# Whole-batch loads of 8 MB through three fixed buffers in a batched row-product and softmax kernel

## The chip, the cores and the metric

The kernel runs on one core of one Trainium2 chip. The metric is the device time of one execution in microseconds (us), the median of several. The profile's span is about 2 us shorter than that time. VectorE is called DVE in the profile's lines, ScalarE ACT, GpSimd POOL, and SP is the engine whose queue issues the loads (SPq).

## The reference

```python
B, N, D = 8, 4096, 512                       # x, y: (B, N, D) float32, 64 MiB each
gram = np.matmul(x, y.transpose(0, 2, 1))
diag = np.diagonal(gram, axis1=1, axis2=2)   # one product-sum over D per row
diag = diag - diag.max(axis=-1, keepdims=True)
exp = np.exp(diag)
return exp / exp.sum(axis=-1, keepdims=True) # softmax over the N rows of a batch
```

Only the diagonal is wanted, so each row of x is multiplied with the same row of y and summed. The 134.22 MB of input are read once.

## The kernel before

A batch lies in SBUF, the memory on the chip that the engines read, as 128 partitions of 32 rows. The kernel works in half batches: 16 rows of x and 16 of y, each a 4 MB load that gives every partition one run of 32 KB. Three x tiles and three y tiles rotate.

```python
H = R // 2                                             # R = 32 rows per partition
io = ctx.enter_context(tc.tile_pool(name="io", bufs=3))
...
def load(b, r0, parts):
    xt = io.tile([P, H, D], f32, tag="xt", name="xt")
    yt = io.tile([P, H, D], f32, tag="yt", name="yt")
    ...
        nc.sync.dma_start(out=xt[:, o : o + n, :], in_=xv[b, :, r0 + o : r0 + o + n, :])
        nc.sync.dma_start(out=yt[:, o : o + n, :], in_=yv[b, :, r0 + o : r0 + o + n, :])
...
def dots(b, r0, xt, yt):
    nc.vector.tensor_tensor(out=xt, in0=xt, in1=yt, op=mybir.AluOpType.mult)
    nc.vector.tensor_reduce(out=diag[:, c : c + H], in_=xt, axis=X, op=add)
...
for b in range(B):
    for h in range(2):
        parts = {2 * B - 2: [8, 8], 2 * B - 1: [8, 4, 2, 1, 1]}.get(n, [H])
        xt, yt = load(b, h * H, parts)
        (dots_by_row if n >= 2 * B - 3 else dots)(b, h * H, xt, yt)
    softmax(b)                                         # after every batch, in DVE's order
```

`dots_by_row` makes one fused multiply-and-sum per row. `softmax` takes the maximum on DVE, reduces it over the partitions on POOL, exponentiates on ACT, sums on POOL, scales on DVE and stores the batch from ACT's queue.

## Time and profile before

| | before |
|---|---|
| time, median (range) | 323.7 us (323.36 to 323.76, 3 runs) |
| load queue, share of the 16 DMA engines' span | 97.5% |
| mean rate over the span | 418 GB/s |
| DVE busy | 81% |

The lines below are from the page of the kernel before. The rows of digits and rates are the span in 40 slices of 8 us.

```profile
span 321.6 us, 345 instructions
DVE 261.4 (81%) x154; ACT 4.6 (1%) x17; POOL 6.1 (2%) x20
...
DVE  0019979898998979979799897989979799776494
...
DMA  8999999999999999999999999999999999999991
GB/s 326 456 395 452 440 408 456 391 458 391 456 412 436 454 395 456 440 408 458 416 432 456 392 458 440 408 456 417 433 449 395 456 437 412 424 424 426 427 407 53
...
q1 hardware_dynamic: 6048, 134.22, 97.5%
```

The DMA row is 9 from the second slice to the one before last: the DMA engines never run dry. The queue line (packets, MB, share) gives 6048 packets. In the trace's DMA records, a packet of 32 KB takes 1213 ns, so 16 engines can carry 16 x 32768 B / 1213 ns = 432 GB/s. The Trainium skill ("DMA: Bandwidth & Descriptors", Where 436 GB/s comes from) puts the ceiling of the 16 SBUF ports at 435.2 GB/s; the trace agrees within 1%. There is little to win here except packet overhead and the two edges.

Why the queue never runs dry is seen from the next lines: the sizes and the median time from issue to landing (the moment when the last of the 16 engines has reported its part done) of the 4 MB loads, and the issues of SP's queue in a stretch of the timeline (start us, us).

```profile
xt<-in_x_dram SPq DMA_DIRECT2D x14, 4096.0 KB, 31.2
yt<-in_y_dram SPq DMA_DIRECT2D x14, 4096.0 KB, 40.5
```

### The profile page before, as it was taken

How to read it: one execution, taken by the hardware profiler on the slowest of the kernel's cores; microseconds unless marked ns; L12 is line 12 of the kernel's file. 1: busy time of each engine (PE TensorE's matmuls, PEld its weight loads, DVE VectorE, ACT ScalarE, POOL GpSimd, SP SyncE). 2: the span in 40 equal slices, each digit the busy share in tenths (PEclk: the TensorE clock that was granted, in tenths of full speed). 3: DMA queues.
4: the chain of work that ended last, by engine and by line, in shares of the span. 5: the costliest groups of instructions: out<-in, count | busy, mean ns of one | idle time of the engine just before them, and what ended most of it. 6: DMA issues, size and time to landing. Idle time of an engine off the chain costs nothing.

```text
span 321.6 us, 345 instructions
## 1 busy us (share of the span) xinstructions
DVE 261.4 (81%) x154; ACT 4.6 (1%) x17; POOL 6.1 (2%) x20
## 2 busy tenths in 40 slices
DVE  0019979898998979979799897989979799776494
ACT  1000000000000000000000000000000000000000
POOL 0000000000000000000000000000000000000000
DMA  8999999999999999999999999999999999999991
GB/s 326 456 395 452 440 408 456 391 458 391 456 412 436 454 395 456 440 408 458 416 432 456 392 458 440 408 456 417 433 449 395 456 437 412 424 424 426 427 407 53
DMA packets 7201, 134.36 MB, mean 418 GB/s; under 512 B 1824, under 2 KB 1824, under 8 KB 2592
## 3 DMA queue, kind: packets, MB, share of 16 engines
q1 hardware_dynamic: 6048, 134.22, 97.5%
q10 hardware_dynamic: 1152, 0.13, 0.3%
q14 instruction: 1, 0.01, 0.0%
HBM read 134.22 MB, written 0.13 MB: 418 GB/s over the span
## 4 chain that ended last, share of the span: by engine, by line
DMA 63%; DVE 33%; issue 1%; SPq 1%; POOL 1%; ACT 0%; POOLq 0%; DVEq 0%
DMA yt<-in_y_dram 63%; DVE xt L50 16%; DVE diag L51 16%; SPq L43 1%; POOL mx L74 0%; POOL ssum L83 0%; DVE mxp L72 0%; DVE xt L58 0%; ACT res L78 0%; DVE rc L85 0%; POOLq L121 0%; SPq L44 0%; DVE res L86 0%; DVE nmx L76 0%; DVEq L50 0%
## 5 line engine op out<-in xcount | busy, mean ns | idle before, releaser
L50 DVE TENSOR_TENSOR xt<-xt,yt 128x8192 f32<-128x8192 f32 x13 | 113.0, 8689 | 34.5 <-DMA yt<-in_y_dram 34.5
L51 DVE TENSOR_REDUCE diag<-xt 128x16 f32<-128x8192 f32 x13 | 112.9, 8686 | 0.4
L58 DVE SCALAR_TENSOR_TENSOR xt<-xt,yt 128x512 f32<-128x512 f32 x48 | 30.0, 687 | 9.9 <-DMA yt<-in_y_dram 9.7
L74 POOL PARTITION_ALL_REDUCE mx<-mxp x8 | 2.8, 352 | 306.6 <-DVE mxp L72 306.6
L85 DVE RECIPROCAL rc<-ssum 128x1 f32<-128x1 f32 x8 | 1.3, 164 | 7.7 <-POOL ssum L83 7.7
L78 ACT ACTIVATE res<-diag,nmx 128x32 f32<-128x32 f32 x8 | 2.6, 321 | 312.9 <-DVE nmx L76 312.9
L76 DVE TENSOR_SCALAR nmx<-mx 128x1 f32<-128x1 f32 x8 | 1.2, 154 | 4.3 <-POOL mx L74 4.3
L58 DVE DVE_READ_ACCUMULATOR xt<-xt,yt 128x1 f32 x48 | 3.9, 82 | 0.0
L83 POOL PARTITION_ALL_REDUCE ssum<-sump x8 | 3.1, 385 | 5.8 <-ACT res L78 5.8
L86 DVE TENSOR_SCALAR res<-res,rc 128x32 f32<-128x32 f32 x8 | 1.9, 242 | 0.9
L72 DVE TENSOR_REDUCE mxp<-diag 128x1 f32<-128x32 f32 x8 | 1.5, 186 | 0.3
L78 ACT ACTIVATION_READ_ACCUMULATOR res<-diag,nmx 128x1 f32 x8 | 1.5, 186 | 0.0
L78 ACT ACT_TABLE_LOAD x1 | 1.3, 1283 | 0.7 <-PEq L110 0.7
L110 POOL MEMSET const-float32-0.0<- 128x1 f32 x1 | 0.1, 100 | 0.2 <-issue 0.2
L110 POOL MEMSET const-bfloat16-1.0<- 128x1 bf16 x1 | 0.1, 102 | 0.0
L110 POOL MEMSET const-uint8-127<- 128x1 uint8 x1 | 0.1, 102 | 0.0
L110 POOL MEMSET const-float32-1.0<- 128x1 f32 x1 | 0.1, 99 | 0.0
## 6 DMA issues: line engine op xcount, KB each, us to landing
xt<-in_x_dram SPq DMA_DIRECT2D x14, 4096.0 KB, 31.2
yt<-in_y_dram SPq DMA_DIRECT2D x14, 4096.0 KB, 40.5
xt<-in_x_dram SPq DMA_DIRECT2D x3, 2048.0 KB, 27.1
yt<-in_y_dram SPq DMA_DIRECT2D x3, 2048.0 KB, 31.6
xt<-in_x_dram SPq DMA_DIRECT2D x1, 1024.0 KB, 31.9
yt<-in_y_dram SPq DMA_DIRECT2D x1, 1024.0 KB, 29.5
xt<-in_x_dram SPq DMA_DIRECT2D x1, 512.0 KB, 25.8
yt<-in_y_dram SPq DMA_DIRECT2D x1, 512.0 KB, 22.2
```

The lines of the kernel that those rows point to most:

```text
L43: nc.sync.dma_start(out=xt[:, o : o + n, :], in_=xv[b, :, r0 + o : r0 + o + n, :])
L50: nc.vector.tensor_tensor(out=xt, in0=xt, in1=yt, op=mybir.AluOpType.mult)
L51: nc.vector.tensor_reduce(out=diag[:, c : c + H], in_=xt, axis=mybir.AxisListType.X, op=mybir.AluOpType.add)
L58: nc.vector.scalar_tensor_tensor(out=xt[:, k, :], in0=xt[:, k, :], scalar=1.0, in1=yt[:, k, :], op0=mybir.AluOpType.mult, op1=mybir.AluOpT ...
L72: nc.vector.tensor_reduce(out=mxp, in_=db, axis=mybir.AxisListType.X, op=mybir.AluOpType.max)
L74: nc.gpsimd.partition_all_reduce(out_ap=mx, in_ap=mxp, channels=P, reduce_op=bass_isa.ReduceOp.max)
L76: nc.vector.tensor_single_scalar(out=nmx, in_=mx, scalar=-1.0, op=mybir.AluOpType.mult)
L78: nc.scalar.activation(out=rb, in_=db, func=mybir.ActivationFunctionType.Exp, bias=nmx, scale=1.0, accum_out=sump,)
L83: nc.gpsimd.partition_all_reduce(out_ap=ssum, in_ap=sump, channels=P, reduce_op=bass_isa.ReduceOp.add)
L85: nc.vector.reciprocal(out=rc, in_=ssum)
L86: nc.vector.tensor_single_scalar(out=rb, in_=rb, scalar=rc, op=mybir.AluOpType.mult)
L110: nc = _bacc.Bacc("TRN2", target_bir_lowering=False, num_devices=1)
```

## The change

The intent is longer runs (64 KB per partition, hence fewer packets), fewer instructions, and no softmax stalls in DVE's order. Whole batches of 8 MB go through three fixed buffers of 64 KB per partition: two for x, one for y. The product overwrites x. Two whole batches of both operands would be 256 KB per partition; the change keeps to the 192 KB that the six tiles took before, so y has only one buffer. The softmax of batches 0 to 4 and of 5 and 6 is done in groups. Batches 6 and 7 are done by row.

```diff
-    H = R // 2
+    wide = B - 2
...
-    io = ctx.enter_context(tc.tile_pool(name="io", bufs=3))
+    xs = [big.tile([P, R, D], f32, name=f"xs{i}") for i in range(2)]
+    ys = big.tile([P, R, D], f32, name="ys")
...
+    def load_x(b, r0, n):
+        nc.sync.dma_start(out=xs[b % 2][:, r0 : r0 + n, :], in_=xv[b, :, r0 : r0 + n, :])
+
+    def load_y(b, r0, n):
+        nc.sync.dma_start(out=ys[:, r0 : r0 + n, :], in_=yv[b, :, r0 : r0 + n, :])
+
+    def dots_wide(b):
+        xt = xs[b % 2]
+        nc.vector.tensor_tensor(out=xt, in0=xt, in1=ys, op=Alu.mult)
+
+    def sums_wide(b):
+        nc.vector.tensor_reduce(out=diag[:, b, :], in_=xs[b % 2], axis=X, op=Alu.add)
...  (group_exp, group_out, last_softmax: the softmax in groups, and of the last batch)
-    for b in range(B):
-        for h in range(2):
-            n = 2 * b + h
-            parts = {2 * B - 2: [8, 8], 2 * B - 1: [8, 4, 2, 1, 1]}.get(n, [H])
-            xt, yt = load(b, h * H, parts)
-            (dots_by_row if n >= 2 * B - 3 else dots)(b, h * H, xt, yt)
-        softmax(b)
+    for b in range(wide):
+        load_x(b, 0, R)
+        load_y(b, 0, R)
+        dots_wide(b)
+        if b == wide - 1:
+            group_out("a", 0, wide - 1, first)
+        sums_wide(b)
+        if b == wide - 2:
+            first = group_exp("a", 0, wide - 1)
+
+    b = B - 2
+    load_x(b, 0, R)
+    for r0 in (0, R // 2):
+        load_y(b, r0, R // 2)
+        for r in range(r0, r0 + R // 2):
+            dot_row(b, r)
+
+    b = B - 1
+    r0 = 0
+    for n in (8, 8, 8, 4, 2, 1, 1):
+        load_x(b, r0, n)
+        load_y(b, r0, n)
+        for r in range(r0, r0 + n):
+            if r == 2:
+                second = group_exp("b", B - 3, 2)
+            if r == 10:
+                group_out("b", B - 3, 2, second)
+            dot_row(b, r)
+        r0 += n
+    last_softmax(b)
```

More of the change, by code (lines that the diff above doesn't have):

```diff
@@ L19 @@
     nc = tc.nc
+    ctx.enter_context(tc.manual_schedule())
     f32 = mybir.dt.float32
+    Alu = mybir.AluOpType
+    Act = mybir.ActivationFunctionType
+    X = mybir.AxisListType.X
     B, N, D = x.shape
@@ L23 @@
     R = N // P
-    H = R // 2
+    wide = B - 2
     xv = x.rearrange("b (p r) d -> b p r d", p=P)
     yv = y.rearrange("b (p r) d -> b p r d", p=P)
-    ov = out.rearrange("b (p r) -> b p r", p=P)
-    io = ctx.enter_context(tc.tile_pool(name="io", bufs=3))
-    persist = ctx.enter_context(tc.tile_pool(name="persist", bufs=1))
-    sm = ctx.enter_context(tc.tile_pool(name="sm", bufs=2))
-    diag = persist.tile([P, B * R], f32, name="diag")
-    res = persist.tile([P, B * R], f32, name="res")
@@ L38, in load @@
-    def load(b, r0, parts):
-        xt = io.tile([P, H, D], f32, tag="xt", name="xt")
-        yt = io.tile([P, H, D], f32, tag="yt", name="yt")
-        o = 0
-        for n in parts:
-            nc.sync.dma_start(out=xt[:, o : o + n, :], in_=xv[b, :, r0 + o : r0 + o + n, :])
-            nc.sync.dma_start(out=yt[:, o : o + n, :], in_=yv[b, :, r0 + o : r0 + o + n, :])
-            o += n
-        return xt, yt
-    def dots(b, r0, xt, yt):
-        c = b * R + r0
-        nc.vector.tensor_tensor(out=xt, in0=xt, in1=yt, op=mybir.AluOpType.mult)
-        nc.vector.tensor_reduce(
-            out=diag[:, c : c + H], in_=xt, axis=mybir.AxisListType.X, op=mybir.AluOpType.add
-        )
@@ L55, in dots_by_row @@
-    def dots_by_row(b, r0, xt, yt):
-        for k in range(H):
-            c = b * R + r0 + k
-            nc.vector.scalar_tensor_tensor(
-                out=xt[:, k, :],
-                in0=xt[:, k, :],
-                scalar=1.0,
-                in1=yt[:, k, :],
-                op0=mybir.AluOpType.mult,
-                op1=mybir.AluOpType.mult,
-                accum_out=diag[:, c : c + 1],
-            )
-    def softmax(b):
-        db = diag[:, b * R : (b + 1) * R]
-        rb = res[:, b * R : (b + 1) * R]
-        mxp = sm.tile([P, 1], f32, tag="mxp", name="mxp")
-        nc.vector.tensor_reduce(out=mxp, in_=db, axis=mybir.AxisListType.X, op=mybir.AluOpType.max)
-        mx = sm.tile([P, 1], f32, tag="mx", name="mx")
-        nc.gpsimd.partition_all_reduce(out_ap=mx, in_ap=mxp, channels=P, reduce_op=bass_isa.ReduceOp.max)
-        nmx = sm.tile([P, 1], f32, tag="nmx", name="nmx")
-        nc.vector.tensor_single_scalar(out=nmx, in_=mx, scalar=-1.0, op=mybir.AluOpType.mult)
-        sump = sm.tile([P, 1], f32, tag="sump", name="sump")
-        nc.scalar.activation(
-            out=rb, in_=db, func=mybir.ActivationFunctionType.Exp,
-            bias=nmx, scale=1.0, accum_out=sump,
-        )
-        ssum = sm.tile([P, 1], f32, tag="ssum", name="ssum")
@@ new lines, with column @@
+    ov = out.rearrange("b (p r) -> p b r", p=P)
+    big = ctx.enter_context(tc.tile_pool(name="big", bufs=1))
+    small = ctx.enter_context(tc.tile_pool(name="small", bufs=1))
+    xs = [big.tile([P, R, D], f32, name=f"xs{i}") for i in range(2)]
+    ys = big.tile([P, R, D], f32, name="ys")
+    diag = small.tile([P, B, R], f32, name="diag")
+    res = small.tile([P, B, R], f32, name="res")
+    def column(name, n):
+        return small.tile([P, n], f32, name=name)
+    def load_x(b, r0, n):
+        nc.sync.dma_start(out=xs[b % 2][:, r0 : r0 + n, :], in_=xv[b, :, r0 : r0 + n, :])
@@ new lines, in load_y, with dot_row @@
+    def load_y(b, r0, n):
[5 more added lines that the diff above has]
+        nc.vector.tensor_reduce(out=diag[:, b, :], in_=xs[b % 2], axis=X, op=Alu.add)
+    def dot_row(b, r):
+        xt = xs[b % 2]
+        nc.vector.scalar_tensor_tensor(
+            out=xt[:, r, :],
+            in0=xt[:, r, :],
+            scalar=1.0,
+            in1=ys[:, r, :],
+            op0=Alu.mult,
+            op1=Alu.mult,
+            accum_out=diag[:, b, r : r + 1],
+        )
@@ new lines, in group_exp @@
+    def group_exp(name, b0, n):
+        mxp, mx, nmx, sump, ssum = (column(name + s, n) for s in ("mxp", "mx", "nmx", "sump", "ssum"))
+        nc.vector.tensor_reduce(out=mxp, in_=diag[:, b0 : b0 + n, :], axis=X, op=Alu.max)
+        nc.gpsimd.partition_all_reduce(out_ap=mx, in_ap=mxp, channels=P, reduce_op=bass_isa.ReduceOp.max)
+        nc.scalar.mul(nmx, mx, -1.0)
+        for i in range(n):
+            nc.scalar.activation(
+                out=res[:, b0 + i, :], in_=diag[:, b0 + i, :], func=Act.Exp,
+                bias=nmx[:, i : i + 1], scale=1.0, accum_out=sump[:, i : i + 1],
+            )
+        nc.gpsimd.partition_all_reduce(out_ap=ssum, in_ap=sump, channels=P, reduce_op=bass_isa.ReduceOp.add)
+        return ssum
@@ new lines, in group_out, with last_softmax @@
+    def group_out(name, b0, n, ssum):
+        rc = column(name + "rc", n)
+        nc.vector.reciprocal(out=rc, in_=ssum)
+        for i in range(n):
+            rb = res[:, b0 + i, :]
+            nc.scalar.activation(out=rb, in_=rb, func=Act.Copy, scale=rc[:, i : i + 1])
+        nc.scalar.dma_start(out=ov[:, b0 : b0 + n, :], in_=res[:, b0 : b0 + n, :])
+    def last_softmax(b):
+        db, rb = diag[:, b, :], res[:, b, :]
+        mxp, mx, nmx, sump, ssum, rc = (column("l" + s, 1) for s in ("mxp", "mx", "nmx", "sump", "ssum", "rc"))
+        nc.vector.tensor_reduce(out=mxp, in_=db, axis=X, op=Alu.max)
+        nc.gpsimd.partition_all_reduce(out_ap=mx, in_ap=mxp, channels=P, reduce_op=bass_isa.ReduceOp.max)
+        nc.vector.tensor_single_scalar(out=nmx, in_=mx, scalar=-1.0, op=Alu.mult)
+        nc.scalar.activation(out=rb, in_=db, func=Act.Exp, bias=nmx, scale=1.0, accum_out=sump)
@@ L83, in softmax @@
         nc.gpsimd.partition_all_reduce(out_ap=ssum, in_ap=sump, channels=P, reduce_op=bass_isa.ReduceOp.add)
-        rc = sm.tile([P, 1], f32, tag="rc", name="rc")
         nc.vector.reciprocal(out=rc, in_=ssum)
-        nc.vector.tensor_single_scalar(out=rb, in_=rb, scalar=rc, op=mybir.AluOpType.mult)
-        nc.scalar.dma_start(out=ov[b], in_=rb)
-    for b in range(B):
-        for h in range(2):
-            n = 2 * b + h
-            parts = {2 * B - 2: [8, 8], 2 * B - 1: [8, 4, 2, 1, 1]}.get(n, [H])
-            xt, yt = load(b, h * H, parts)
-            (dots_by_row if n >= 2 * B - 3 else dots)(b, h * H, xt, yt)
-        softmax(b)
+        nc.vector.tensor_single_scalar(out=rb, in_=rb, scalar=rc, op=Alu.mult)
@@ new lines, in last_softmax @@
+        nc.scalar.dma_start(out=ov[:, b, :], in_=rb)
+    for b in range(wide):
[14 more added lines that the diff above has]
+    b = B - 1
```

## The prediction

> **What bounds the kernel now.** The load queue. The queue table gives 134.22 MB at 97.5% of the 16 DMA engines' span of 321.6 us. In the DMA records a 32 KB packet takes 1213 ns (median), a 16 KB packet 612 ns: 601 ns per 16 KB plus about 11 ns per packet, so 16 engines carry 16 x 32768 B / 1213 ns = 432 GB/s. The Trainium skill ("DMA: Bandwidth & Descriptors", Where 436 GB/s comes from) names a 435.2 GB/s port ceiling; the trace agrees. In stretches of 10 us the DMA share is 0.97 to 1.07 from 10 us to about 310 us: there is no hole to fill. The chain of waits reads the same way: DMA yt 63%; the DVE pieces in it (33%) only freed buffers whose loads queued behind others. VectorE is busy 81% and waits for yt 44 us.
>
> Edges: first packet 1.4 us after the first issue; last y piece lands at 316.1, then one row, softmax and store to 321.6 (timeline). The call adds 2.1 us.
>
> **What the change does.**
> 1. Bytes: the same; 8.39 MB per DMA engine at 601 ns per 16 KB is 307.7 us. That floor is not touched.
> 2. Packets: about 336 per DMA engine before, about 232 after (64 KB for six and a half batches). At 11 ns each, 1.2 us saved, all on the critical path, if a 64 KB run travels as one packet.
> 3. Three buffers, one y. Estimates: multiply and sum over 16384 elements take 2 x 8.69 minus 0.15 = 17.2 us each. y(b+1) can be issued only when multiply b ends, 17.3 us after y(b) landed, and its first packet follows 1.3 to 1.45 us later (last store and first load): at 18.65 to 18.75. x(b+1) keeps the DMA engines busy until 18.9 to 19.3 (19.33 us per 8 MB; engines finish within 0.43 us of each other). So y arrives just in time, with 0.2 to 0.6 us to spare. I expect holes of 0 to 0.5 us at six handovers: 1 us in total. x(b+1) waits for sums b-1, and is 4 us early.
> 4. Batches 6 and 7 by row: 64 rows at a pace of 0.612 us (timeline) are 39.2 us. After y(5), VectorE needs 34.6 + 39.2 + about 1 = 75 us; the loads need about 78. The end stays DMA-bound, with 3 us of slack.
> 5. Softmax groups: eight in-order stalls of about 2.3 us leave VectorE, but it was waiting for DMA anyway. The last softmax and store are the same.
>
> **Sum.** 321.6 - 1.2 + 1 = 321.4 us of span, about 323.2 us. Predicted 323.0 us, 80% range 321.0 to 326.5. Faster by over 2%: 2%; within 2%: 93%; slower by over 2%: 5%.
>
> **What would show each step.** Load packets falling from 6048 to about 4200, with 64 KB packets near 2415 ns; if runs are cut in two, no saving. Load queue share 97 to 98%, 418 to 420 GB/s. Each y issue 17.3 us after the previous y landing, x-to-y gaps under 0.5 us in the packet starts. y(5) landing near 236 us, last y near 315 to 316. VectorE waiting only for DMA at the end.
>
> **What would make it wrong.** An idle DMA engine that restarts slowly: the program's first packets took up to 1.95 us instead of 1.21; such a restart at six handovers would cost 5 us. A wait for a whole y buffer instead of its rows in batch 7 would cost 15 us or more. GpSimd reductions delayed by VectorE, so that a reciprocal blocks the row products. VectorE later than estimated at the end, making the tail compute-bound.

## More of the kernel before

Every run named here is a fast one at a granted clock of 1.0.

```profile
176.61 0.33 SPq L43 DMA_DIRECT2D xt<-in_x_dram  x1
177.03 0.38 SPq L44 DMA_DIRECT2D yt<-in_y_dram  x1
196.32 0.33 SPq L43 DMA_DIRECT2D xt<-in_x_dram  x1
196.70 0.42 SPq L44 DMA_DIRECT2D yt<-in_y_dram  x1
```

A 4 MB load needs 9.7 us of the DMA engines' time, but it takes 31 to 41 us from issue to landing: it stands in the queue behind two or three others. That is about 20 to 30 us of work ahead of every load. A late multiply cannot be felt.

## The result

| | before | after |
|---|---|---|
| time, median (range) | 323.65 us (323.36 to 323.76, 4 runs) | 331.65 us (330.63 to 332.73, 4 runs) |
| ratio | | 1.0249 (1.0216 to 1.0282) |
| load packets | 6048 | 4176 |
| load queue share | 97.5% | 95.5% |

A ratio is the mean time of one kernel's fast runs over that of the other's of the same rounds, so it is not quite the ratio of the medians. The changed kernel is 2.5% slower, outside the predicted range of 321.0 to 326.5 us.

The page of the kernel after, the lines that answer to those of before:

```profile
span 331.0 us, 298 instructions
DVE 247.6 (75%) x148; ACT 6.2 (2%) x26; POOL 3.3 (1%) x10
...
DVE  0000099992999949999399983999829999999584
...
DMA  9898998998999898899999899898999799999992
GB/s 380 380 507 380 451 436 380 388 491 388 483 396 388 380 499 388 380 436 444 396 459 396 380 396 491 380 388 380 388 499 388 305 401 446 406 425 434 419 414 71
...
q1 hardware_dynamic: 4176, 134.22, 95.5%
```

The packets fell as planned, and DVE has less to do. But the DMA row now has ten 8s and one 7. (Not every 8 is a hole: a packet of 64 KB is counted whole in the slice where it starts, which also makes the rates jump. The run e1 below has three 8s and a 7 without the loss.) The sums are surer: the load queue's busy time is 0.955 x 331.0 = 316 us against 0.975 x 321.6 = 314 us, while the span grew by 9.4 us. In the DMA records a DMA engine was without a packet for 7.3 us between the first packet and the last, against 0.5 before (mean of the 16). So of the 9.4 us about 7 are holes and 2.6 are in the packets, whose time grew although fewer packets should have shrunk it by a microsecond; the reason comes below.

The time from issue to landing of the whole-batch y loads (the size column is blank in this view):

```profile
ys<-in_y_dram SPq DMA_DIRECT2D x6, 23.8
```

An 8 MB load needs 19.33 us of the DMA engines' time. So y no longer stands behind two or three other loads: from its issue to its landing it takes only 2 to 5 us more than its own transfer (21.8 to 24.3 us in the five handovers shown below).

Where the dips lie is seen in the chain of waits of the kernel after (start us, us, what), cut to the pieces of interest:

```profile
42.14 17.24 DVE xs L55
...
59.40 23.53 DMA ys<-in_y_dram
...
100.28 21.78 DMA ys<-in_y_dram
...
139.40 23.37 DMA ys<-in_y_dram
...
180.11 24.05 DMA ys<-in_y_dram
...
221.51 24.32 DMA ys<-in_y_dram
```

Between these pieces stands each time the same 17.24 us multiply. (The Trainium skill, "VectorE: DVE Perf Modes", Walkthrough, mode 1x, has a float32 multiply of two tensors at one element a cycle of 0.96 GHz; for 16384 elements that would be 17.07 us, an estimate from the page, and the trace agrees with 17.23.) So the loop is closed: y lands, the multiply runs, the next y is issued, y lands. Before the change, the pieces of this chain that DVE held freed buffers whose loads waited behind others anyway; here the loads wait for DVE. The timeline of the kernel after shows the order of the issues (in brackets DVE's idle time before the instruction and what ended it):

```profile
83.02 17.23 DVE L55 TENSOR_TENSOR xs<-xs,ys 128x16384 f32<-128x16384 f32 x1 [6.40 <-DMA ys<-in_y_dram]
100.28 0.33 SPq L51 DMA_DIRECT2D ys<-in_y_dram  x1
100.28 17.22 DVE L58 TENSOR_REDUCE diag<-xs 128x32 f32<-128x16384 f32 x1
117.53 0.33 SPq L48 DMA_DIRECT2D xs<-in_x_dram  x1
122.14 17.23 DVE L55 TENSOR_TENSOR xs<-xs,ys 128x16384 f32<-128x16384 f32 x1 [4.64 <-DMA ys<-in_y_dram]
```

The y load is issued the moment the multiply ends, never earlier. The Trainium skill ("DMA: Bandwidth & Descriptors", Anatomy of one DMA, written of DMAs issued from GpSimd) says that DMA engines do not wait on semaphores and that any such wait is the issuing sequencer's, before dispatch. The trace agrees: the issue at 100.28 follows the multiply's end within 0.03 us, and until then nothing of that load is in the queue.

### What the DMA records say of a handover

A handover is the moment when the DMA engines are through with x of a batch and go on to its y. The trace's DMA records hold the start, length and size of every packet, but not its engine; each engine's last record of a load is a small completion, so the 16 ends of an x load and the 16 first packets of the following y can be read. A 64 KB packet that follows another without a stall took 2.42 us in every run. Counted from the issue of y in the kernel after:

```
handover (y issued at)   x ends, first..last engine   first y packet starts   it takes (us)
 59.40 (y of batch 1)     1.06 ..  1.63                1.21 .. 2.94            2.70 .. 3.49
100.28 (y of batch 2)    -0.31 ..  2.07                0.95 .. 2.07            2.42 .. 3.45
139.40 (y of batch 3)     1.13 ..  1.68                1.34 .. 3.31            2.42 .. 3.09
180.11 (y of batch 4)    -0.49 ..  1.87                0.96 .. 3.59            2.83 .. 3.40
221.51 (y of batch 5)    -0.98 ..  1.81                0.95 .. 3.40            2.55 .. 3.64
```

These times are on the trace's own clock, which packets and instructions share: the profile of the kernel after has no packet from 0.72 to 1.70 us and the first ones from 1.70 to 1.80, so 1.0 us after the first issue at 0.72. The recorded texts place the DMA records 0.41 to 0.44 us later than that. Their "1.4 us" and "1.3 to 1.45 us" from issue to first packet, and their ends of x counted from an issue ("3.7 to 4.4 us", "2.56 us"), are to be read as that much less. A landing, which is read from the semaphores, comes about 0.35 us after the last record of its load.

At 59.40 the spare was what I had predicted. I had 0.2 to 0.6 us between y's first possible packet and the end of x; x ended at 1.06 to 1.63, and the earliest start seen on a dry engine is 0.95 (at 100.28), so it was 0.1 to 0.7 us. Yet no engine went on smoothly. All sixteen first packets were stretched by 0.3 to 1.1 us, and three engines started 0.5 to 1.2 us later than the rest. So y landed 21.55 us after x in place of 19.33. The stretched packets count as busy, so the DMA row shows only a part of the loss.

The delay also feeds on itself: the next multiply starts when the slowest engine has landed, so the faster engines are through with the following x before the next y can reach them (x ends from 0.11 us on at 100.28 and from -0.06 us on at 180.11).

Landing to landing, y of batches 1 to 5 came 2.22, 0.07, 2.01, 2.51 and 2.82 us later than 19.33 us after x: 9.6 us in five handovers. At 100.28 the cost was nearly nothing because the slowest engine, the one that counts, had not run dry (its first y packet took 2.42 us).

### The profile page after: what moved, and what is told of

The parts are those of the page before. It is cut to its first block, busy times and chain, and to the rows that moved or that the text cites. A ratio compares the mean times of both kernels' runs of the same rounds, so it can differ in the third digit from the quotient of the medians.

```text
span 331.0 us, 298 instructions
## 1 busy us (share of the span) xinstructions
DVE 247.6 (75%) x148; ACT 6.2 (2%) x26; POOL 3.3 (1%) x10
## 3 DMA queue, kind: packets, MB, share of 16 engines
q1 hardware_dynamic: 4176, 134.22, 95.5%
## 4 chain that ended last, share of the span: by engine, by line
DMA 58%; DVE 39%; issue 2%; SPq 0%; POOLq 0%; ACT 0%; POOL 0%; DVEq 0%; ACTq 0%
DMA ys<-in_y_dram 54%; DVE xs L55 31%; DVE diag L58 4%; DVE xs L62 4%; DMA out_dram<-res 3%; SPq L48 0%; POOLq L161 0%; ACT res L91 0%; POOL lmx L98 0%; DVE res L103 0%; DVE lmxp L97 0%; DVE lrc L102 0%; DVEq L55 0%; DVE arc L88 0%; DVE brc L88 0%
## 5 line engine op out<-in xcount | busy, mean ns | idle before, releaser
L55 DVE TENSOR_TENSOR xs<-xs,ys 128x16384 f32<-128x16384 f32 x6 | 103.4, 17226 | 73.2 <-DMA ys<-in_y_dram 73.2
L58 DVE TENSOR_REDUCE diag<-xs 128x32 f32<-128x16384 f32 x6 | 103.3, 17220 | 0.2
L62 DVE SCALAR_TENSOR_TENSOR xs<-xs,ys 128x512 f32<-128x512 f32 x64 | 39.8, 688 | 6.0 <-DMA ys<-in_y_dram 5.9
L62 DVE DVE_READ_ACCUMULATOR xs<-xs,ys 128x1 f32 x64 | 5.3, 83 | 0.0
L91 ACT ACTIVATE res<-res,arc 128x32 f32<-128x32 f32 x5 | 1.2, 310 | 21.9 <-DVE arc L88 21.9
L79 ACT ACTIVATE res<-diag,anmx 128x32 f32<-128x32 f32 x5 | 1.5, 309 | 0.0
L76 POOL PARTITION_ALL_REDUCE bmx<-bmxp x1 | 0.7, 735 | 59.4 <-DVE bmxp L75 59.4
L79 ACT ACTIVATION_READ_ACCUMULATOR res<-diag,anmx 128x1 f32 x5 | 0.9, 187 | 0.0
L83 POOL PARTITION_ALL_REDUCE bssum<-bsump x1 | 0.8, 797 | 1.1 <-ACT res L79 1.1
```

Of the source, the lines that this page charges most:

```text
L55: nc.vector.tensor_tensor(out=xt, in0=xt, in1=ys, op=Alu.mult)
L58: nc.vector.tensor_reduce(out=diag[:, b, :], in_=xs[b % 2], axis=X, op=Alu.add)
L62: nc.vector.scalar_tensor_tensor(out=xt[:, r, :], in0=xt[:, r, :], scalar=1.0, in1=ys[:, r, :], op0=Alu.mult, op1=Alu.mult, accum_out=diag ...
L76: nc.gpsimd.partition_all_reduce(out_ap=mx, in_ap=mxp, channels=P, reduce_op=bass_isa.ReduceOp.max)
L79: nc.scalar.activation(out=res[:, b0 + i, :], in_=diag[:, b0 + i, :], func=Act.Exp, bias=nmx[:, i : i + 1], scale=1.0, accum_out=sump[:, i ...
L83: nc.gpsimd.partition_all_reduce(out_ap=ssum, in_ap=sump, channels=P, reduce_op=bass_isa.ReduceOp.add)
```

## The experiments

The theory (A): the loss is y reaching a queue that is about to run dry, because its one buffer is freed only by the end of a 17.2 us multiply. Its stricter form (A2): an engine must have the next packet in its queue for some time before it finishes the last one; being there just before is not enough. Rivals: (A1) plain lateness, each tenth late costs a tenth; (B) the 64 KB packets themselves; (C) the softmax groups and the fixed order.

All kernels gave correct results. The median times of "before" in the same rounds were 323.40 to 323.49 us (323.65 for the changed kernel).

| run | y issued, against the changed kernel | time, median (range), us | over before (95%) |
|---|---|---|---|
| e5_y_halves | about 18 us earlier | 322.60 (322.54 to 323.10) | 0.9980 (0.9967 to 0.9992) |
| e1_y_last4_apart | 4.6 us earlier | 322.56 (322.42 to 322.72) | 0.9973 (0.9958 to 0.9988) |
| e9_y_last2_apart | 2.5 us earlier | 322.74 (322.51 to 323.11) | 0.9975 (0.9961 to 0.9988) |
| e2_y_last1_apart | 1.2 us earlier | 328.00 (326.23 to 329.85) | 1.0142 (1.0100 to 1.0184) |
| the changed kernel | 0 | 331.65 (330.63 to 332.73) | 1.0249 (1.0216 to 1.0282) |
| e8_y_1us_later | 1.1 us later | 331.37 (331.02 to 331.57) | 1.0243 (1.0229 to 1.0257) |
| e4_y_2us_later | 2.2 us later | 337.59 (337.54 to 337.82) | 1.0440 (1.0423 to 1.0458) |

The shifts are the time from the landing of all of y to the issue of the next y, less the 17.35 us that it takes in the changed kernel, on the mean of the handovers (e9: 2.3 to 2.9). The time without a packet, per engine as above, goes with them: 1.1 us in e5, 0.4 in e1, 0.6 in e9, 3.2 in e2, 7.3 in the changed kernel, 6.7 in e8, 12.6 in e4, and 5.6 in e3, where y waits as in the changed kernel.

### e1_y_last4_apart: y earlier, packets as long

```diff
-        nc.vector.tensor_tensor(out=xt, in0=xt, in1=ys, op=Alu.mult)
+        for r0, r1 in ((0, 28), (28, R)):
+            nc.vector.tensor_tensor(
+                out=xt[:, r0:r1, :], in0=xt[:, r0:r1, :], in1=ys[:, r0:r1, :], op=Alu.mult)
...
-        load_y(b, 0, R)
+        load_y(b, 0, 28)
+        load_y(b, 28, R - 28)
```

> Batches 0-5 load y as 28 rows and 4 rows, and multiply in the same two pieces, so the big y load of the next batch can be issued about 4.5 us earlier (it waits only for the 28-row multiply, which itself starts 2.4 us earlier). Runs of y become 56 KB and 8 KB, x keeps 64 KB. Theory A (the holes come from a y load that reaches a queue about to run dry; a DMA engine needs its next packet queued some 2 us ahead to go on without a stall): the handover delays vanish, y(5) lands near 236.5 us instead of 245.9, time 321.5 to 323.5 us. Rival B (the long runs or packets of 56 to 64 KB make the 16 DMA engines drift apart or stall): holes stay, 329 to 333 us. Rival C (the softmax groups or the fixed order cost the time): stays at 331 us.

322.56 us: the whole loss is gone, and the second y piece of batch 5 landed at 236.0 us (my prediction for y of batch 5 was 236; the changed kernel had 245.8). The page and the timeline of this run:

```profile
span 320.6 us, 318 instructions
...
DMA  9998999899999999979999999999899999999991
...
q1 hardware_dynamic: 5040, 134.22, 97.4%
```

```profile
117.26 17.29 DVE L56 TENSOR_TENSOR xs<-xs,ys 128x14336 f32<-128x14336 f32 x2 [4.23 <-DMA ys<-in_y_dram]
132.38 2.53 SPq L51 DMA_DIRECT2D ys<-in_y_dram  x2
134.59 17.22 DVE L61 TENSOR_REDUCE diag<-xs 128x32 f32<-128x16384 f32 x1
151.84 0.33 SPq L48 DMA_DIRECT2D xs<-in_x_dram  x1
```

The y issue (132.38) now comes 2.2 us before the multiply of all rows ends. In the DMA records, x ended 5.62 to 6.18 us after it, every engine's first y packet began within 0.02 us of that, and all took 2.12 us, the unstalled time of 56 KB. B and C fall as causes: packets of 56 and 64 KB and the groups are all still there.

### e2_y_last1_apart and e9_y_last2_apart: how early is early enough

The same edit with 31 + 1 and 30 + 2 rows.

> As the run with 4 rows apart, but 31 rows and 1 row: the big y load is issued only about 1.1 to 1.2 us earlier than after the change. If the cost is only that y is queued a few tenths of a us too late (A1: plain lateness, 0.1 to 0.3 us as my 1.4 us from issue to first packet had it), 1.1 us is more than enough: 321.5 to 323.5 us. If an engine needs the next packet queued about 2 us ahead (A2: restart), the holes shrink but stay: 325 to 329 us. Rivals B and C: 330 to 333 us.

> 30 rows and 2 rows: the big y load is issued about 2.3 us earlier than in the changed kernel, so x should end 3.7 to 4.4 us after that issue. In the 1-row run no stall was seen where x ended 2.56 us or more after the issue. Theory A2 (an issue some 2 to 2.5 us ahead of need is enough): no stalled first packets, 322.4 to 323.5 us, as with 4 rows apart. If the lead needed is longer than that (over 3.5 us): 325 us or more.

With 1.2 us more lead the loss shrank but did not vanish (328.00 us), so A1 falls: by plain lateness 1.2 us would have been ample for a shortfall of tenths. With 2.5 us more lead it vanished (322.74 us), and 4.6 and 18 us more gave nothing further. The records give the threshold, counted from y's issue:

```
run, handover          x ends, first..last    first y packet starts   it takes (unstalled)
2 rows apart, 135.46    3.15 .. 3.90           3.15 .. 3.90            2.27 all (2.27)
1 row apart,   58.25    2.17 .. 2.88           2.16 .. 2.87            13 at 2.34, others up to 3.39 (2.34)
1 row apart,   98.08    1.26 .. 2.79           1.26 .. 3.89            2.34 .. 2.78 (2.34)
changed,       59.40    1.06 .. 1.63           1.21 .. 2.94            2.70 .. 3.49 (2.42)
```

So y has to be issued some 2 to 3 us before an engine runs out, of which 0.95 us is the way from the issue to a first packet. The threshold is not sharp: three of the engines at 58.25 stalled although x ended 2.7 us or more after the issue, and at 98.08 two did not although x ended at 1.9 and 2.0. So my words in the expectation of the 2-row run, that no stall was seen from 2.56 us on (2.16 on the trace's clock), were too strong. In the 2-row run x ended 3.1 us or more after the issue at all five handovers, and none of the first packets was stalled.

### e3_runs_of_32k: the packets short again, the wait kept

```diff
-        load_x(b, 0, R)
-        load_y(b, 0, R)
+        for r0 in (0, R // 2):
+            load_x(b, r0, R // 2)
+        for r0 in (0, R // 2):
+            load_y(b, r0, R // 2)
```

> The same three buffers, waits and order; only each 8 MB load of batches 0-5 is cut in two of 4 MB, so packets are 32 KB as before the change. Both y halves still wait for the whole multiply. Theory A: the holes stay; time 330 to 334 us (1.2 us of packet overhead comes back). Rival B (64 KB packets at fault): back to 322 to 325 us.

331.40 us (330.83 to 333.19), ratio 1.0256 (1.0227 to 1.0285): equal to the changed kernel. The length of the runs is not the cause. This and e1 together settle B.

### e4_y_2us_later and e8_y_1us_later: the other direction

```diff
         nc.vector.tensor_tensor(out=xt, in0=xt, in1=ys, op=Alu.mult)
+        nc.vector.tensor_reduce(out=waste[:, 0:4], in_=ys[:, 0:4, :], axis=X, op=Alu.max)
```

(With 0:2 in e8. The result is not used.)

> After each whole-batch multiply VectorE runs one more reduction over 4 rows of y (about 2.3 us, its result unused), so every y load of batches 1 to 6 is issued 2.3 us later. Theory A: each of six handovers grows by about 2.3 us, less what slack is left: 340 to 346 us. If the holes do not come from y's issue time (B, C): under 335 us.

> After each whole-batch multiply one more reduction over 2 rows of y: y is issued about 1.1 us later than in the changed kernel. Linear lateness (each us later costs a us at each of six handovers): 336 to 339 us. What the run 2.3 us later showed (a y load takes 21.85 us from issue to landing when all 16 DMA engines are already dry, but 21.8 to 24.3 us, mean 23.4, when it comes just as they run dry): period 17.34 + 1.1 + 21.9 = 40.3 us against 40.8 now, so no slower than the changed kernel: 329 to 333 us.

e4 came out at 337.59 us, below what I expected: 2.2 us at each handover cost 5.9 us in all, not the 8 to 14 us that 340 to 346 us meant. The chain of waits of e4 shows why:

```profile
59.10 2.21 DVE waste L57
61.33 21.82 DMA ys<-in_y_dram
...
102.69 21.70 DMA ys<-in_y_dram
...
143.93 21.92 DMA ys<-in_y_dram
...
185.39 21.75 DMA ys<-in_y_dram
```

When all DMA engines are already dry, y takes 21.7 to 22.0 us from issue to landing every time. In the changed kernel it took 21.78 to 24.32, 23.4 on the mean. An issue 1 to 2 us before the engines run dry, too late to be smooth and too early to be a plain restart, is the worse case: in the changed kernel the last engine's first y packet started 2.9 to 3.6 us after the issue at four of the five handovers, in e4 and e8 by 2.2 us in all. From this the e8 expectation: 1.1 us later, a period of 17.34 + 1.1 + 21.9 = 40.3 us, hence no slower. It measured 331.37 us, equal to the changed kernel, with y issued within 0.5 us of the end of x, y landing 21.7 to 22.0 us after its issue, and 40.3 us from y landing to y landing (changed: 40.8, e4: 41.4, e1: 38.8, before: 39.0). So the cost of a late load here is a dry restart of about 2.5 us (21.85 less 19.33; 0.95 us of it before the first packet) plus a penalty of up to 2.5 us for near misses. Why first packets are stretched, and why one to three engines start so much later in a near miss, no run settles.

### e5_y_halves and e10_halves_longer_tail_runs: a version better than both

Two halves of 16 rows in place of 28 + 4; and the same with batch 7 in pieces of (16, 8, 4, 2, 1, 1) rows.

> As the run with 4 rows apart, but y and the multiply in two halves of 16 rows: the first half of the next y is free far earlier (about 18 us before the changed kernel's issue, then held only by the order of the queue). The packets per DMA engine are as many as with 4 rows apart. Theory A (once y is queued more than 2 us ahead, more lead buys nothing): 322.2 to 322.9 us, equal to e1_y_last4_apart (322.56). If lead or earlier VectorE work were still worth something: under 321.5.

> A try at a version better than both: e5_y_halves with batch 7 in pieces of 16, 8, 4, 2, 1, 1 rows in place of 8, 8, 8, 4, 2, 1, 1: 16 packets per DMA engine fewer and two loads fewer, 0.2 us; VectorE should still keep up at 0.612 us a row against 1.21 us of loading a row. 322.1 to 322.7 us; above 323.0 would mean that VectorE falls behind at the end.

322.60 us and 322.57 us (322.44 to 322.66; ratio 0.9969, 0.9955 to 0.9982): the same as e1. More lead buys nothing, and the longer pieces at the end nothing that can be seen. These versions are faster than the kernel before by 0.2 to 0.3%, with intervals clear of 1, and than the changed kernel by 2.7%.

### e6_lead_short_runs: what the long runs are worth

On top of e1:

```diff
-        load_x(b, 0, R)
-        load_y(b, 0, 28)
+        for r0 in (0, R // 2):
+            load_x(b, r0, R // 2)
+        for r0 in (0, 14):
+            load_y(b, r0, 14)
```

> e1_y_last4_apart with every x load cut in two of 16 rows and the big y load in two of 14 rows: 96 more packets per DMA engine and 12 more loads, waits unchanged. At 11 ns per packet and 9 ns per completion: 1.1 us more than e1, about 323.6 to 323.8 us, that is, equal to the kernel before within 0.2 us. If the long runs buy nothing: equal to e1 (322.5).

323.93 us (323.85 to 324.07), ratio 1.0018 (1.0005 to 1.0030): 1.4 us more than e1. The gain that the change was made for is real, and the estimate of 11 ns per packet was near; it is also about all of it, since the version with short runs is no faster than the kernel before.

### e7_lead_softmax_by_batch: what the groups are worth

On top of e1, `last_softmax(b)` after the sums of every batch in place of the two groups.

```diff
-        if b == wide - 1:
-            group_out("a", 0, wide - 1, first)
         sums_wide(b)
-        if b == wide - 2:
-            first = group_exp("a", 0, wide - 1)
+        last_softmax(b)
```

(And the same for batch 6, whose group went out of the loop of batch 7.)

> e1_y_last4_apart with the softmax of every batch in VectorE's order right after its sums, as before the change, in place of the groups. VectorE idles about 4 us per batch waiting for y and a softmax stalls it 2.3 us: within 0.4 us of e1 (322.2 to 323.0). If the groups were needed: 324 us or more.

323.06 us (322.94 to 323.30), ratio 0.9991 (0.9978 to 1.0003): 0.5 us over e1 and just over my range. In its records y of batch 5 lands 0.45 us later than in e1, spread over the loads; a small store of each batch now runs beside the loads. That the stores are the reason is argued, not shown. The groups are worth half a microsecond at most here and have no part in the loss.

## Why the prediction was wrong

- **The bound (right).** The load queue was and is the limit. When y is queued early, the same three-buffer kernel ends at 322.56 us.
- **Steps 1 and 2, bytes and packets (right).** 4176 packets against "about 4200"; a 64 KB packet took 2418 ns in the median against 2415; the long runs are worth 1.4 us (e6 less e1) against 1.2.
- **Step 3, the one y buffer (wrong in size; this is the step that failed).** The prediction's words: "So y arrives just in time, with 0.2 to 0.6 us to spare. I expect holes of 0 to 0.5 us at six handovers: 1 us in total." The spare was right: the multiply took 17.23 us against 17.2, and at the first handover x ended 0.1 to 0.7 us after y's first packet could have come. (Both of these times were placed about 0.4 us too late, which cancels in the difference.) The term that was mis-sized is the cost of arriving just in time: 9.6 us in five handovers, not 1 us; the sixth cost nothing more. I had taken a packet that is in the queue before the engine runs out as a packet that costs nothing. Moving y's issue 2.5 us earlier removes the cost (e9), 1.2 us removes 40% of it (3.65 of the 9.1 us between the changed kernel and e1).
- **The warning (right in kind, half in size).** "An idle DMA engine that restarts slowly ... such a restart at six handovers would cost 5 us" is what happened, but I gave it too little weight and sized it from the stretch of one packet (0.75 us). The runs show about 2.5 us for a fully dry restart and up to 5 us for a near miss, both over the 19.33 us of work, and a near miss makes the next one likelier because the slowest engine sets the next issue.
- **Step 4, the end (nearly right).** From y of batch 5 to the last landing took 79.7 us in the changed kernel, against 78; before it was 79.3, so the short pieces at the end were undersized by about 1.5 us in both kernels. The end stayed bound by the loads: DVE's last wait of note there is for y. No whole-buffer wait came up in batch 7.
- **Step 5, the groups (right).** Worth 0.5 us at most (e7).

With the mis-sized term put right, the sum of the prediction (321.6 - 1.2 + 9.6, and 2 us for the call) gives 332 us against the 331.65 measured.

## What to carry to other kernels

How early a load is issued is worth more than how long its runs are: ask for every load how much work stands in the queue before it at the moment of its issue, and keep that above 3 us or so as measured here, not above zero. When a single large buffer is freed by one long instruction, cut the instruction and the load that follows into two pieces (28 + 4 rows did as well as 16 + 16); the buffers can stay. A DMA busy share that drops by only two points is not small: here it stood for 7 us of holes. The stalled packets count as busy and hid the rest, so compare a packet's duration at the handover with its usual one.

## What the Trainium skill lacked or had wrong

- "DMA: Bandwidth & Descriptors" has a rule to issue a DMA early so that its fixed cost overlaps, and one that asks for 1 MiB per DMA and 128 partitions for full bandwidth. It does not say how early. Here 8 MB loads over 128 partitions lost 9.6 us in five handovers although their issue led the engines' end by 1.1 to 1.6 us at the first of them; 3.1 us of lead was enough (e9), 2.2 us nearly (first handover of e2).
- The same page (Latency and other measured facts) gives about 600 ns to the first byte for loads from SP's queue. It does not say from when that is counted. In these traces the first packet on a dry engine started 0.95 us after the start of the issue, which is about 0.62 us after the end of the 0.33 us issue instruction: the page's figure agrees if it is counted from that end. It does not say either that this first packet is slow: in the restarts of e4 most took 0.4 to 1.1 us longer than a later one.
- No page says that a load that is issued 1 to 2 us before the engines run dry lands later after its issue (23.4 us on the mean in the changed kernel) than one that is issued 0.5 to 1.3 us after they ran dry (21.7 to 22.0 us, e4). Making every y load 1.1 us later cost nothing (331.37 against 331.65 us).
- The same page (Why small descriptors are slow) gives a fixed overhead of about 3 cycles per packet, on the example of 256 B, and no figure for long runs. For these, the traces give 8 to 11 ns a packet (612, 1213 and 2418 ns for 16, 32 and 64 KB), worth 1.4 us in this kernel (e6).
